# Half A's feed-forward in half B's order: its second product partly by blocks, and eight weight-sum jobs moved beside its later couples

## The chip, the cores and the metric

The kernel runs on one core of one Trainium2 chip. The metric is the device time of one execution in microseconds; the time of a kernel is the median of its runs.

## The reference

One layer of a decoder, on 1024 prompt tokens and 32 sample tokens (8 sequences of 4) that share the weights; a second conditioning of the same form goes with the samples. All is float32. Cut to what matters here:

```
h  = rmsnorm(x) * (1 + sc1) + sh1
u  = h @ w_in                                  # x, gate, q, k, v, r, low rank, two merge gates
y_a = rg_lru(conv(u_x)) * gelu(u_g)            # D_RNN 1280, ten blocks of 128
y_b = rmsnorm(chunked_gla(q, k, v, g)) * silu(u_r)
m  = sigmoid(u_ga) * (y_a @ proj_a) + sigmoid(u_gb) * (y_b @ proj_b)
x  = x + gt1 * (m @ w_out)
h2 = rmsnorm(x) * (1 + sc2) + sh2
f1, f2 = split(h2 @ ffn_w1)                    # 1024 -> 2 x 2816
x  = x + gt2 * ((silu(f1) * f2) @ ffn_w2)      # 2816 -> 1024
```

The outputs are the normalised x and the new states of the convolution, the RG-LRU and the GLA.

## The kernel before

**Halves and products.** The tokens are worked in two halves, one after the other: half A (names end in a) is the first 512 prompt tokens, half B (names in b) the other 512 and the 32 samples. Activations lie transposed, features on partitions, tokens in the free dimension. Each float32 product is three TensorE matmuls of split parts (high by high, high by low, low by high). A weight tile is loaded by SP's queue into one of five raw buffers, and `split_w` (L151) makes the parts in one of three "hl" buffers: a copy on ScalarE (L154) and a subtraction on VectorE (L155).

**The feed-forward.** The 2816 hidden features are 22 tiles of 128, each made by a couple of weight tiles (`ffn1`, one column tile for f1 and one for f2). In the whole form (`pair`, `ffn2`) a product is matmuls of 512 columns, three for each k-tile. In the block form (`ffn1_fast`, `ffn2_fast`, with `products` at L1410) a 2 x 2 block scheme makes seven half-size products instead of eight; a couple is then 7 x 4 x 3 = 84 matmuls of 256 columns (tiles fapsa, fbpsa, fcpsa) in place of 96 halves, and the four output couples of `ffn2_fast` are 4 x 7 x 3 x 3 = 252 matmuls (tiles that print as gapsa, gbpsa and gcpsa, like the gates of merge_a; L1472, on six k-tiles). The block form needs sums of the activations (`block_sums`, and `keep` for the hidden tiles) and sums of the weights.

**The weight sums.** They are made while half A runs and stored in device memory, for half A's last couples, for half B's first product (wsum, one for each couple), for its gates (wsumg) and for its second product (wsumf). Two generators make them, one step at each `next` in the places that the main program chooses:

- `weight_sums` (L348), the raw jobs: SP loads two tiles of 128 x 1024, VectorE makes four sums of 128 x 512 (L352 to L355), POOL's queue stores both.
- `paced_sums` (L362), the half-size jobs: POOL copies one column of a pace tile into each of two buffers (L387), which holds the load back to a place in the program; POOL's queue loads both (L388), VectorE makes four sums of 128 x 256 or 128 x 384 (L392 to L396), POOL's queue stores both (L398). The buffers are the tag "sums", two in all, so one job takes both; the copy also waits for the old store from its buffer. The first sum takes the tile that is loaded second.

**Order.** The order on each engine is the order of the code, shaped by generators that are mixed (`mix`, `weave`) and by `high_priority`, which lets splits and some ScalarE copies move ahead. VectorE, ScalarE, POOL and SP each work through their queue in order. Large activations live in 17 slots of the pool "S", smaller ones in 8 of the pool "X" (`xp`).

**Half A before.** `merge_b` (L1182) makes eight columns of gate and y_b product; between them the generator `lru` finishes the last RG-LRU blocks, with the root of blocks 8 and 9 (L1155) and the scan (L1129). `merge_a` (L1271) makes eight columns of gate (gapsa) and y_a product (papsa, two weight tiles pa0a and pa1a). `back` (L1618) does w_out, the norm and the feed-forward: couples 0 to 5 whole (`ffn1_first`, `ffn1`, tiles f1psa, f2psa, f1psa4None ...), couples 6 to 10 by blocks, the whole `ffn2` of k-tiles 0 to 10 (tile f3psa), and from the main program couples 11 to 21 by blocks, then `ffn2` of k-tiles 11 to 21. Half B has in its `back` one `ffn2` of k-tiles 0 to 3 and then `ffn2_fast` twice.

**Jobs before.** Raw jobs for couples 6 to 21: at columns 1 to 7 of `merge_b`, at five columns of `merge_a`, and four in the first `ffn2`. Half-size jobs: two steps at each of columns 4 to 7 of half A's `merge_b` (couples 4 and 5), four jobs for wsumf in `merge_a`, and in half B the rest.

Of the kernel before, what the change touches and what calls it, by code (L numbers as in the profile page):

```python
# [15 lines left out]
P = 128  # L16
D = 1024
KD = 8
# [9 lines left out]
LEVELS = (64, 32, 16, 8, 4, 2, 1)  # L28
EPS = 1e-6
EARLY = 4  # L30
FAST = (6, 4)
KF = (3, 2, 1, 0, 4, 6, 8, 5, 7, 9, 10, 12, 14, 11, 13, 15, 16, 17, 18, 19, 20, 21)
KORD = (0, 2, 4, 6, 1, 3, 5, 7)
GATES = KD // 2
# [20 lines left out]
def hybrid_layer(ctx, tc, I, O):  # L55
# [25 lines left out]
    tp = ctx.enter_context(tc.tile_pool(name="tp", bufs=6))  # L81
    axp = ctx.enter_context(tc.tile_pool(name="axp", bufs=2, space=PSUM))
    drp = ctx.enter_context(tc.tile_pool(name="drp", bufs=1, space=bass.MemoryType.DRAM))
    wsum = {f: drp.tile([P, 2048], F32, name=f"wsum{f}") for f in range(FAST[1], NF)}
    wsumg = [drp.tile([P, 2048], F32, name=f"wsumg{c}") for c in range(GATES)]
    wsum2 = {(q, g): drp.tile([P, 1536], F32, name=f"wsumf{q}{g}") for q in range(4) for g in range(2)}

# [3 lines left out]
    def T(name, w=544):  # L91
        return tp.tile([P, w], F32, tag="t", name=name)
# [254 lines left out]

    def weight_sums():  # L348

        for f in range(FAST[0], NF):  # L350
            r1, r2 = load_raw(I["ffn1"][2 * f], 1024, f"s1{f}"), load_raw(I["ffn1"][2 * f + 1], 1024, f"s2{f}")
            dve.tensor_add(r2[:, 512:1024], r2[:, 0:512], r2[:, 512:1024])  # L352
            dve.tensor_sub(r2[:, 0:512], r1[:, 0:512], r2[:, 0:512])
            dve.tensor_sub(r1[:, 0:512], r2[:, 512:1024], r1[:, 0:512])
            dve.tensor_sub(r1[:, 512:1024], r1[:, 512:1024], r1[:, 0:512])  # L355
            pool.dma_start(wsum[f][:, 0:1024], r1)
            pool.dma_start(wsum[f][:, 1024:2048], r2)
            yield 1
# [3 lines left out]
    def paced_sums():  # L362
# [11 lines left out]
                to = [halves(wsum2[q, g][:, v * 768:(v + 1) * 768], 384, 0) for v in range(2)]  # L374
                jobs.append((384, [halves(I["ffn2"][2 * q + v][:, c:c + 768], 384, 0) for v in range(2)], to))

        for f in range(FAST[1], FAST[0]):
            columns(wsum[f], [I["ffn1"][2 * f + v] for v in range(2)])
        rows(0)
        for c in range(GATES):  # L380
            columns(wsumg[c], [I["w_in"][T_GA + 2 * c + v] for v in range(2)])
        rows(1)
# [20 lines left out]
    class Half:  # L403
        def __init__(s, hf):
            s.hf, s.N = hf, WID[hf]
            s.n = "ab"[hf]

            s.whole = (0, s.N, None, None)
            s.parts = [(0, 256, 0, 0), (256, 256, 0, 256)] if hf == 0 else [(0, 272, 0, 0), (272, 272, 1, 0)]
            s.tiled = None if hf == 0 else [(0, 256, 0, 0), (256, 288, 1, 0)]  # L410
            s.halves = s.parts if hf == 0 else [(o, w, 0, 0) for o, w, _, _ in s.parts]
            s.adas = ada_rest() if hf == 0 else iter(())
            s.early = {}
            s.lr_raw = None
# [673 lines left out]
        def lru_gate(s, nb, m, xc):  # L1088
# [8 lines left out]
                for o, p in s.over(t, g):  # L1097
                    act.activation(o, p, AF.Tanh, scale=0.5, bias=vh[:, b:b + 1])
            dve.scalar_tensor_tensor(ti[:, :N], ti[:, :N], 1.0, xc[:, :N], op0=OP.add, op1=OP.mult)
            if s.hf == 0 or nb < NR - 1:  # L1100
                both = S("la" + n)
                a, hh = both[:, :N], both[:, 544:544 + N]
            else:
                a, hh = [xp.tile([P, 544], F32, tag="X", name=k + n)[:, :N] for k in ("la", "lh")]
# [77 lines left out]
        def merge_b(s):  # L1182
# [14 lines left out]
            for j in range(KD):  # L1197
                n = f"{s.n}{j}"
                if j + lag < KD:
                    first(j + lag)  # L1200
                    yield 5.2
                tg = tgs.pop(j)
                p2 = s.wide("pbps" + n)
                s.gemm(p2, load_w(I["proj_b"][j], 1024, "pb" + n), 8, s.y_b)
                m = xp.tile([P, 544], F32, tag="X", name="mb" + n)
                for (t, p), (o, _) in zip(s.over(tg, p2), s.over(m, p2)):
                    dve.scalar_tensor_tensor(o, t, 1.0, p, op0=OP.add, op1=OP.mult)
                s.mb.append(m)
                pace[0] = tg
                if s.hf == 0 and j:  # L1210
                    next(sums_of, None)
                if s.hf or j >= 4:
                    next(sums_late, None)
                    next(sums_late, None)
                yield 5.2

        def gate_a(s, j):
# [53 lines left out]
        def merge_a(s):  # L1271
            s.m = []
            for j in range(KD):
                tg = s.gate_a(j)
                s.join(j, tg, s.over(tg, s.branch_a(j)))
                s.keep_m(j)
                next(sums_late, None)
                if j % 3 < 2 and j < 7:
                    next(sums_of, None)

# [161 lines left out]
        def keep(s, f, tg):  # L1442

            N, W = s.N, s.N // 2
            if not (s.hf and 4 <= f < 16):
                a = s.act[f] = S(f"fa{s.n}{f}", F32R)
                split(a, tg[:, :N], N)
                return
# [23 lines left out]
        def ffn2_fast(s, g):  # L1472
# [11 lines left out]
            def onto(j, v):  # L1484
                x, samples = s.x[j], lambda t: t[:, HP:N].rearrange("p (b t) -> p b t", t=TS)
                dve.scalar_tensor_tensor(x[:, :HP], v[:, :HP], gains[:, 3, j, 0:1], x[:, :HP], op0=OP.mult, op1=OP.add)
                fx = cp.tile([P, NB, TS], F32, tag="fx", name=f"fx{s.n}{g}{j}", bufs=2)
                dve.tensor_mul(fx, samples(v), bc(gains[:, 3, j, 1:9].unsqueeze(2), [P, NB, TS]))
                dve.tensor_add(samples(x), fx, samples(x))
# [26 lines left out]
        def ffn1_fast(s, fs):  # L1516
# [9 lines left out]
            for f in fs:  # L1526
                n = f"{s.n}{f}"
                pa, pb, pc = [mm(f"f{c}ps{n}")[:, 0, :W] for c in "abc"]
                v1, v2 = T("va" + n), T("vb" + n)
                tg = s.kept(f) if s.hf and f < 16 and f % 2 == 0 else T("ft" + n)  # L1530
                hi, lo, nn = slice(0, W), slice(W, N), slice(0, N)
                product(pa, "11", True)
                s.snap(v1[:, lo], pa)
# [2 lines left out]
                product(pa, "t2", False)  # L1536
                s.snap(v1[:, hi], pa)
                product(pb, "22", False)
                yield 6
                product(pa, "t3", False)  # L1540
                s.snap(v2[:, hi], pa)
# [9 lines left out]
                if s.hf and f == 16:  # L1551
                    s.late = tg
                else:
                    s.keep(f, tg)
                yield 4.5
            as_written(begin, (mybir.EngineType.PE,))

        def ffn1_first(s, part, n):
            for f in range(n) if part[0] == 0 else range(n - 1, -1, -1):
                if part[0] == 0:  # L1560
                    s.act[f] = S(f"fa{s.n}{f}", F32R)
                yield from s.pair(f, part, s.act[f])

        def ffn1(s, fs):
            for f in fs:
                a = s.act[f] = S(f"fa{s.n}{f}", F32R)
                yield from s.pair(f, s.whole, a)

        def ffn2(s, k0, k1, part, acc=None):
            chunks = [(c, min(6, k1 - c)) for c in range(k0, k1, 6)]  # L1570
# [47 lines left out]
        def back(s):  # L1618
# [13 lines left out]
            mix(s.norm2(p1, a1), f)  # L1632
            drain(f)
            b = s.block_sums(s.h2)
            if s.hf == 0:
                mix(chain(s.ffn1_first(p1, EARLY), s.ffn1(range(EARLY, FAST[0]))), b)
                drain(b)
                drain(s.ffn1_fast(range(FAST[0], 11)))
                for j, _ in enumerate(s.ffn2(0, 11, s.whole)):
                    if j % 2 == 0:  # L1640
                        next(sums_of, None)
                return
            s.fs = {k: [] for k in ("11", "21", "22", "t1", "t2", "t3", "t4")}
            mix(chain(s.ffn1_first(p1, EARLY), s.ffn2(0, 4, s.whole)), b)
            drain(b)
            drain(s.ffn1_fast(range(4, 11)))
            drain(s.ffn2_fast(0))
            drain(s.ffn1_fast(range(11, 17)))
            drain(s.ffn2_fast(1))
            s.keep(16, s.late)  # L1650
# [39 lines left out]
    derive()  # L1690
    A.branches(None)
    drain(sums_of)
    A.act = {}
    drain(A.ffn1_fast(range(11, NF)))
    acc = [ACC("3a")]
    dn = A.ffn2(11, NF, A.whole, acc)
    next(dn)
    B.load_x(pool)
    mix(chain(B.norm1_sum(), B.norm1()), dn)
# [117 lines left out]
```

## Time and profile before

| what | value |
|---|---|
| time, median of 3 runs (range) | 1961.64 us (1959.43 to 1966.48) |
| the profiled execution: its time, its span | 1964.05 us, 1962.3 us |
| mean granted TensorE clock | 0.994 |
| VectorE busy | 1361.2 us (69%) |
| ScalarE busy | 972.8 us (50%) |
| DMA moved | 319.24 MB, mean 163 GB/s |

The span is from the first to the last instruction. Times in a row are microseconds from the start of the span; a row of the timeline is start, duration, engine, line, operation, output and inputs by the program's names, shapes, and in brackets the idle time of the engine before it with what ended that. TensorE's matmuls are pipelined, so their spacing is told by the starts. A row of the windows is from:to, its length, then the busy time of PE, its weight load, VectorE, ScalarE and POOL, each with its count of instructions, the granted clock as a share of the full one, the share of the DMA engines and GB/s.

### The profile page before, as it was taken

How to read it: one execution, taken by the hardware profiler on the slowest of the kernel's cores; microseconds unless marked ns; L12 is line 12 of the kernel's file. 1: busy time of each engine (PE TensorE's matmuls, PEld its weight loads, DVE VectorE, ACT ScalarE, POOL GpSimd, SP SyncE). 2: the span in 40 equal slices, each digit the busy share in tenths (PEclk: the TensorE clock that was granted, in tenths of full speed). 3: DMA queues.
4: the chain of work that ended last, by engine and by line, in shares of the span. 5: the costliest groups of instructions: out<-in, count | busy, mean ns of one | idle time of the engine just before them, and what ended most of it. 6: DMA issues, size and time to landing. Idle time of an engine off the chain costs nothing. (4 is left out here: it accounts for less than half of the span.)

```text
span 1962.3 us, 33970 instructions
## 1 busy us (share of the span) xinstructions
PE 1928.1 (98%) x13380; PEld 1756.9 (90%) x13380; DVE 1361.2 (69%) x2420; ACT 972.8 (50%) x1559; POOL 148.8 (8%) x279
## 2 busy tenths in 40 slices
PE   9999999998999999999999999999999999999997
PEld 5877777786899998999899998999999999999997
DVE  5648587666658774677674497786467688888867
ACT  4536376533235552555353365665245354666653
POOL 0000001122100000000000001141201000000000
PEclk9999999998999999999999999999999999999999
DMA  8344325476764456554332412334446634555553
GB/s 341 116 154 175 117 92 197 153 262 250 267 227 156 129 179 234 196 185 156 118 119 68 145 50 88 127 121 141 146 140 228 202 130 130 176 169 180 176 164 105
DMA packets 122241, 319.24 MB, mean 163 GB/s; under 512 B 14561, under 2 KB 29665, under 8 KB 122081
## 3 DMA queue, kind: packets, MB, share of 16 engines
q1 hardware_dynamic: 107536, 263.89, 41.5%
q0 software_dynamic: 14000, 52.62, 7.4%
q8 instruction: 105, 1.72, 0.4%
q10 hardware_dynamic: 544, 0.56, 0.1%
q14 instruction: 56, 0.45, 0.1%
HBM read 278.42 MB, written 38.59 MB: 162 GB/s over the span
## 5 line engine op out<-in xcount | busy, mean ns | idle before, releaser
L155 DVE TENSOR_TENSOR fwa_hl<-fwa,fwa_hl 128x1024 fp32r<-128x1024 f32 (+1 forms) x57 | 68.8, 1207 | 44.4 <-ACT fwa_hl L154 43.8
L155 DVE TENSOR_TENSOR fwb_hl<-fwb,fwb_hl 128x1024 fp32r<-128x1024 f32 (+1 forms) x64 | 77.2, 1207 | 27.4 <-ACT fwb_hl L154 27.1
L154 ACT ACTIVATE fwa_hl<-fwa 128x1024 fp32r<-128x1024 f32 (+1 forms) x57 | 59.3, 1040 | 43.7 <-PE fapsa L1431 10.7
L154 ACT ACTIVATE fwb_hl<-fwb 128x1024 fp32r<-128x1024 f32 (+1 forms) x64 | 66.6, 1041 | 23.4 <-PE fcpsb L1431 9.0
L454 PE MATMUL f3psa<-faa,f3a_hl 128*128 128x512 f32 x176 | 68.7, 391 | 1.2 <-DVE f3a_hl L155 1.2
L452 PE MATMUL f3psa<-faa,f3a_hl 128*128 128x512 f32 x176 | 68.7, 390 | 0.6 <-ACT f3a_hl L154 0.6
L453 PE MATMUL f3psa<-faa,f3a_hl 128*128 128x512 f32 x176 | 68.6, 390 | 0.0
L154 ACT ACTIVATE f3a_hl<-f3a_raw 128x768 fp32r<-128x768 f32 (+1 forms) x32 | 25.3, 792 | 56.7 <-PE f3psa L454 37.8
L352 DVE TENSOR_TENSOR s_raw<-s_raw 128x512 f32<-128x512 f32 x16 | 11.1, 692 | 49.3 <-DMA s_raw<-in_ffn 49.3
L454 PEld LDWEIGHTS f3psa<-faa,f3a_hl 128*128 128x128 f32 x176 | 33.0, 188 | 8.9 <-DVE f3a_hl L155 2.1
L452 PEld LDWEIGHTS f3psa<-faa,f3a_hl 128*128 128x128 f32 x176 | 33.0, 188 | 7.7 <-ACT f3a_hl L154 1.0
L453 PEld LDWEIGHTS f3psa<-faa,f3a_hl 128*128 128x128 f32 x176 | 33.1, 188 | 6.8
L155 DVE TENSOR_TENSOR f3a_hl<-f3a_raw,f3a_hl 128x768 fp32r<-128x768 f32 (+1 forms) x32 | 28.3, 888 | 14.3 <-ACT f3a_hl L154 14.3
L454 PE MATMUL wopsb<-mb,wob_hl 128*128 128x272 f32 x128 | 36.9, 288 | 0.0
L452 PE MATMUL wopsb<-mb,wob_hl 128*128 128x272 f32 x128 | 36.9, 289 | 0.0
L453 PE MATMUL wopsb<-mb,wob_hl 128*128 128x272 f32 x128 | 36.8, 288 | 0.0
L453 PE MATMUL wopsa<-ma,woa_hl 128*128 128x256 f32 x128 | 36.4, 284 | 0.0
L454 PE MATMUL wopsa<-ma,woa_hl 128*128 128x256 f32 x128 | 36.2, 283 | 0.0
L452 PE MATMUL wopsa<-ma,woa_hl 128*128 128x256 f32 x128 | 36.1, 283 | 0.0
L1616 POOL DMA_DIRECT2D out_yb<-yb x4 | 2.9, 720 | 407.6 <-DVE yb L1613 406.9
L452 PE MATMUL uxpsa<-h1a,uxpsa_hl 128*128 128x512 f32 x80 | 32.3, 403 | 0.0
L155 DVE TENSOR_TENSOR fvb_hl<-fvb,fvb_hl 128x768 fp32r<-128x768 f32 x28 | 26.8, 956 | 7.7 <-ACT fvb_hl L154 7.3
(2402 smaller groups left out, 7986.7 us busy)
## 6 DMA issues: line engine op xcount, KB each, us to landing
ada<-in_ada_w SPq DMA_DIRECT2D x48, 512.0 KB, 5.5
fwb<-wsum SPq DMA_DIRECT2D x72, 256.0 KB, 3.6
s_raw<-in_ffn SPq DMA_DIRECT2D x32, 512.0 KB, 4.8
wsum<-s_raw POOLq DMA_DIRECT2D x32, 512.0 KB, 3.8
fwa<-wsum SPq DMA_DIRECT2D x64, 256.0 KB, 3.4
fwb<-in_ffn SPq DMA_DIRECT2D x54, 256.0 KB, 3.7
fwa<-in_ffn SPq DMA_DIRECT2D x48, 256.0 KB, 3.2
woa_raw<-in_w_out SPq DMA_DIRECT2D x13, 512.0 KB, 3.6
```

The costliest lines, as they stand in the source:

```text
L154: act.activation(hl[:, 0, :n], raw[:, :n], AF.Copy)
L155: dve.tensor_sub(hl[:, 1, :n], raw[:, :n], hl[:, 0, :n].bitcast(F32))
L352: dve.tensor_add(r2[:, 512:1024], r2[:, 0:512], r2[:, 512:1024])
L452: pe.matmul(out, wh, x[:, o:o + w], start=st, stop=False)
L453: pe.matmul(out, wh, x[:, N + o:N + o + w], start=False, stop=False)
L454: pe.matmul(out, wl, x[:, o:o + w], start=False, stop=en)
L1616: (queues[j // 2 % len(queues)]).dma_start(out[:, j:j + 2, o:o + w], y2)
```

## The change

- **Half A's feed-forward takes half B's order.** `FAST = (6, 4)` becomes `RAW, BLOCKS = (6, 18), (10, 16)`. In `back`, half A now does couples 0 to 3 with the whole `ffn2` of k-tiles 0 to 3, couples 4 to 10 by blocks, and `ffn2_fast(0)` on k-tiles 4 to 9; then the main program does couples 11 to 21 by blocks and the whole `ffn2` of k-tiles 10 to 21. `keep` makes the block parts for half A's tiles 4 to 9.
- **Raw jobs** are those of couples 6 to 17: columns 0 to 6 of `merge_b` and five of `merge_a`. There are none in a whole `ffn2`.
- **Half-size jobs** are two-phase at each place: a first `next` issues the loads, a second, later in the same column or couple, the sums and stores. Those of couples 4 and 5 stand at columns 3 to 6 of `merge_b`, those of wsumf at columns 1 to 4 of `merge_a`. Eight new ones, for couples 18 to 21, stand in the last `ffn1_fast` of half A beside couples 12 to 19, paced by the result of the couple before (`fta`).
- **RG-LRU block 9** of half A has its decay and state (`la`, `lh`) in the pool "X", as half B has, and not in a slot of "S".

The matmuls of the kernel go from 12606 to 12786: f3psa from 528 to 384, the whole couples 4 and 5 from 192 to none, 168 more of a block couple, 252 of the second product.

```diff
-FAST = (6, 4)
+RAW, BLOCKS = (6, 18), (10, 16)
...
-        for f in range(FAST[0], NF):
+        for f in range(*RAW):
...
-        for f in range(FAST[1], FAST[0]):
-            columns(wsum[f], [I["ffn1"][2 * f + v] for v in range(2)])
+        def pairs(fs):
+            for f in fs:
+                columns(wsum[f], [I["ffn1"][2 * f + v] for v in range(2)])
+
+        pairs(range(EARLY, RAW[0]))
         rows(0)
+        pairs(range(RAW[1], NF))
...
-            if s.hf == 0 or nb < NR - 1:
+            if nb < NR - 1:
                 both = S("la" + n)
...
                     first(j + lag)
+                if s.hf or 3 <= j < 7:
+                    pace[0] = tgs[j]
+                    next(sums_late, None)
+                if j + lag < KD:
                     yield 5.2
...
-                pace[0] = tg
-                if s.hf == 0 and j:
+                if s.hf or 3 <= j < 7:
+                    next(sums_late, None)
+                if s.hf == 0 and j < 7:
                     next(sums_of, None)
-                if s.hf or j >= 4:
-                    next(sums_late, None)
-                    next(sums_late, None)
...
                 tg = s.gate_a(j)
+                if 1 <= j < 5:
+                    next(sums_late, None)
                 s.join(j, tg, s.over(tg, s.branch_a(j)))
                 s.keep_m(j)
-                next(sums_late, None)
+                if 1 <= j < 5:
+                    next(sums_late, None)
...
-            if not (s.hf and 4 <= f < 16):
+            if not EARLY <= f < s.blocks:
...
                 product(pb, "22", False)
+                late = s.hf == 0 and 12 <= f < 20
+                if late:
+                    next(sums_late, None)
                 yield 6
...
                     s.keep(f, tg)
+                if late:
+                    next(sums_late, None)
+                pace[0] = tg
                 yield 4.5
...
-            if s.hf == 0:
-                mix(chain(s.ffn1_first(p1, EARLY), s.ffn1(range(EARLY, FAST[0]))), b)
-                drain(b)
-                drain(s.ffn1_fast(range(FAST[0], 11)))
-                for j, _ in enumerate(s.ffn2(0, 11, s.whole)):
-                    if j % 2 == 0:
-                        next(sums_of, None)
-                return
             s.fs = {k: [] for k in ("11", "21", "22", "t1", "t2", "t3", "t4")}
             mix(chain(s.ffn1_first(p1, EARLY), s.ffn2(0, 4, s.whole)), b)
             drain(b)
             drain(s.ffn1_fast(range(4, 11)))
             drain(s.ffn2_fast(0))
+            if s.hf == 0:
+                return
...
-    dn = A.ffn2(11, NF, A.whole, acc)
+    dn = A.ffn2(10, NF, A.whole, acc)
```

In the changed kernel the lines behind L402 are four to fourteen higher; L392 to L398 of the half-size jobs are L396 to L402 there, and L1550 is L1564.

**ScalarE at the end of half A's merge_b.** laa is the decay of RG-LRU block 9 (lma holds the squares of blocks 8 and 9 for the root), gba a gate of merge_b, pa0a and pa1a the weights of merge_a's first column. Before:

```order
L1098 ACTIVATE tia_3418<-g2a_3414,vh 128x512
L1192 ACTIVATE gba_3458<-gbpsa_3428 128x512
...
L154 ACTIVATE pa0a_hl<-pa0a_raw 128x640
L1106 ACTIVATE laa_3422<-tra_3417,sp_147 128x512
L1192 ACTIVATE gba_3630<-gbpsa_3600 128x512
L1107 ACTIVATE tra_3417<-tra_3417,sp_147 128x512
L1108 ACTIVATE lma_3394<-laa_3422 128x512
L1155 ACT_TABLE_LOAD
L1155 ACTIVATE lma_3394<-lma_3394 128x1024
L154 ACTIVATE pa1a_hl<-pa1a_raw 128x640
```

And now:

```order
L1102 ACTIVATE tia_3440<-g2a_3436,vh 128x512
L1110 ACTIVATE laa_3444<-tra_3439,sp_147 128x512
L1111 ACTIVATE tra_3439<-tra_3439,sp_147 128x512
L1112 ACTIVATE lma_3416<-laa_3444 128x512
L1159 ACT_TABLE_LOAD
L1159 ACTIVATE lma_3416<-lma_3416 128x1024
L1196 ACT_TABLE_LOAD
L1196 ACTIVATE gba_3481<-gbpsa_3451 128x512
```

The decay, the square and the root moved from between the two weight splits of merge_a's first column to ahead of the gate that is the second row before.

**VectorE in the last ffn1_fast of half A.** fta is the result of a couple, faa its kept split, fwa_hl the split of the next weights, vaa and vba parts of the next couple. From the result of couple 12 on, before:

```order
L1550 TENSOR_TENSOR fta_7029<-fta_7029,fapsa_7024 128x256
L155 TENSOR_TENSOR fwa_hl<-fwa_7252,fwa_hl 128x1024
L189 TENSOR_TENSOR faa_7143<-fta_7029,faa_7143 128x512
L1542 TENSOR_TENSOR vaa_7149<-vaa_7149,fbpsa_7147 128x256
L155 TENSOR_TENSOR fwa_hl<-fwa_7293,fwa_hl 128x1024
L1545 TENSOR_TENSOR vba_7150<-vba_7150 128x256
```

And now:

```order
L1564 TENSOR_TENSOR fta_7326<-fta_7326,fapsa_7321 128x256
L155 TENSOR_TENSOR fwa_hl<-fwa_7567,fwa_hl 128x1024
L189 TENSOR_TENSOR faa_7446<-fta_7326,faa_7446 128x512
L396 TENSOR_TENSOR sums_7391<-sums_7391 128x256
L1556 TENSOR_TENSOR vaa_7458<-vaa_7458,fbpsa_7456 128x256
L398 TENSOR_TENSOR sums_7391<-sums_7390,sums_7391 128x256
L155 TENSOR_TENSOR fwa_hl<-fwa_7614,fwa_hl 128x1024
L399 TENSOR_TENSOR sums_7390<-sums_7391,sums_7390 128x256
L1559 TENSOR_TENSOR vba_7459<-vba_7459 128x256
L400 TENSOR_TENSOR sums_7390<-sums_7390 128x256
```

The four sums of a job now stand in the queue behind the keep, the first of them ahead of the next weight split.

**POOL's queue in the same stage.** xb is half B's input, wsum_92 to wsum_95 the stores of couples 18 to 21. Before, from the first whole ffn2 on:

```order
L357 DMA wsum_94<-s_raw 128x1024
L356 DMA wsum_94<-s_raw 128x1024
L357 DMA wsum_95<-s_raw 128x1024
L356 DMA wsum_95<-s_raw 128x1024
L541 DMA xb_8321<-in_xb 128x1088
```

And now, the first two of the eight jobs:

```order
L391 COPY sums_7390<-fta_7198 128x1
L391 COPY sums_7391<-fta_7198 128x1
L392 DMA sums_7390<-in_ffn 128x2x256
L392 DMA sums_7391<-in_ffn 128x2x256
L402 DMA wsum_92<-sums_7391 128x2x256
L402 DMA wsum_92<-sums_7390 128x2x256
L391 COPY sums_7524<-fta_7326 128x1
L392 DMA sums_7524<-in_ffn 128x2x256
L391 COPY sums_7525<-fta_7326 128x1
L392 DMA sums_7525<-in_ffn 128x2x256
```

The loads of a job stand behind the stores of the job before, each behind a copy into its own buffer.

More of the change, by code (lines that the diff above doesn't have):

```diff
@@ L83, in hybrid_layer @@
     drp = ctx.enter_context(tc.tile_pool(name="drp", bufs=1, space=bass.MemoryType.DRAM))
-    wsum = {f: drp.tile([P, 2048], F32, name=f"wsum{f}") for f in range(FAST[1], NF)}
+    wsum = {f: drp.tile([P, 2048], F32, name=f"wsum{f}") for f in range(EARLY, NF)}
     wsumg = [drp.tile([P, 2048], F32, name=f"wsumg{c}") for c in range(GATES)]
@@ L405, in __init__ @@
             s.hf, s.N = hf, WID[hf]
-            s.n = "ab"[hf]
+            s.n, s.blocks = "ab"[hf], BLOCKS[hf]
             s.whole = (0, s.N, None, None)
@@ L1529, in ffn1_fast @@
                 v1, v2 = T("va" + n), T("vb" + n)
-                tg = s.kept(f) if s.hf and f < 16 and f % 2 == 0 else T("ft" + n)
+                tg = s.kept(f) if f < s.blocks and f % 2 == 0 else T("ft" + n)
                 hi, lo, nn = slice(0, W), slice(W, N), slice(0, N)
@@ L1562, in ffn1_first @@
                 yield from s.pair(f, part, s.act[f])
[L1564 to L1567, printed above, removed]
         def ffn2(s, k0, k1, part, acc=None):
@@ L1647, in back @@
             drain(s.ffn2_fast(0))
+            if s.hf == 0:
+                return
             drain(s.ffn1_fast(range(11, 17)))
@@ L1692, in hybrid_layer @@
     drain(sums_of)
-    A.act = {}
     drain(A.ffn1_fast(range(11, NF)))
     acc = [ACC("3a")]
-    dn = A.ffn2(11, NF, A.whole, acc)
+    dn = A.ffn2(10, NF, A.whole, acc)
     next(dn)
```

## Prediction

> **What bounds the kernel now.** I read the page's busy times and slices first, then TensorE's own rows in order of time, then the DMA view and the rows of one job. The page:
>
> ```profile
> span 1962.3 us, 33970 instructions
> PE 1928.1 (98%) x13380; PEld 1756.9 (90%) x13380; DVE 1361.2 (69%) x2420; ACT 972.8 (50%) x1559; POOL 148.8 (8%) x279
> PE   9999999998999999999999999999999999999997
> PEclk9999999998999999999999999999999999999999
> ```
>
> TensorE is busy for 98% of the span, so a change pays in two ways only: fewer TensorE microseconds, or less of the 34 us in which it waits. In the slices PE and its clock both fall short in the tenth alone (442 to 491 us). There stands the one large gap, between the two projections of half A's merge_a, column 0. TensorE's rows at it, and those of the next column beside them:
>
> ```profile
> 458.11 0.39 PE L452 MATMUL papsa<-yaa,pa0a_hl 128*128 128x512 f32 x1
> 469.74 0.80 PE L454 MATMUL papsa<-yaa,pa1a_hl 128*128 128x512 f32 x1 [7.48 <-DVE pa1a_hl L155]
> 475.46 0.52 PE L452 MATMUL gapsa<-h1a,gapsa_hl 128*128 128x512 f32 x1
> 481.05 0.39 PE L452 MATMUL papsa<-yaa,pa0a_hl 128*128 128x512 f32 x1
> 487.85 0.39 PE L452 MATMUL gapsa<-h1a,gapsa_hl 128*128 128x512 f32 x1
> 452.00:482.00 30.00, 22.52 (x87) 17.87 (x86) 20.81 (x33) 11.58 (x15) 13.56 (x16) 0.83 0.59 200
> ```
>
> Column 0 takes 475.46 - 458.11 = 17.35 us, column 1 takes 487.85 - 481.05 = 6.80 us for the same matmuls: the gap costs **10.6 us**, 7.48 of it idle and the rest at the lower granted clock (0.83 in the window's row) behind it. Who was late, on ScalarE and VectorE:
>
> ```profile
> 456.66 0.60 ACT L1192 ACTIVATE gba<-gbpsa 128x512 f32<-128x512 f32 x1 [7.73 <-DVE mba L1207]
> 459.79 1.06 ACT L1155 ACTIVATE lma<-lma 128x1024 f32<-128x1024 f32 x1
> 460.76 0.72 ACT L154 ACTIVATE pa1a_hl<-pa1a_raw 128x640 fp32r<-128x640 f32 x1
> 463.75 0.43 DVE L392 TENSOR_TENSOR sums<-sums 128x256 f32<-128x256 f32 x1 [3.95 <-DMA sums<-in_ffn]
> 468.87 0.82 DVE L155 TENSOR_TENSOR pa1a_hl<-pa1a_raw,pa1a_hl 128x640 fp32r<-128x640 f32 x1
> ```
>
> ScalarE reaches the square root of LRU blocks 8 and 9 (L1155) late, behind a gate (L1192) that waited 7.73 us; VectorE then waits 3.95 us for the load of a half-size job, and only after that do the scan and the split of pa1a follow.
>
> **The change part by part.** First the two products that move to blocks, from the starts of TensorE's matmuls:
>
> ```profile
> 659.37 0.40 PE L452 MATMUL f1psa4None<-h2a,f1a4None_hl 128*128 128x512 f32 x1
> 681.16 0.28 PE L1429 MATMUL fapsa<-h2a,fwa_hl 128*128 128x256 f32 x1
> 792.41 0.28 PE L1429 MATMUL fapsa<-h2a,fwa_hl 128*128 128x256 f32 x1
> 903.06 0.40 PE L452 MATMUL f3psa<-faa,f3a_hl 128*128 128x512 f32 x1
> ```
>
> Couples 4 and 5 are now 96 matmuls of 512 columns in 681.16 - 659.37 = 21.79 us, 0.227 each. The last 11 couples by blocks take (903.06 - 792.41)/11 = 10.06 us each: 84 matmuls, 0.1197 each.
>
> - Couples 4 and 5 by blocks: 2 x 10.06 - 21.79 = **-1.7 us**.
> - Second product: k-tiles 4 to 9 leave the whole form, 144 x 0.227 = 32.7 us, and come back as 252 half-width matmuls, 30.2 us: **-2.5 us**. Its own weight sums are four jobs that were done already, now in merge_a.
> - The gap: block 9 of half A no longer waits for a slot of the large pool, so its exponential, root and scan stand ahead of the last gate in the order, and no job is summed between column 7 of merge_b and column 0 of merge_a. I take the whole gap as gone: **-10.6 us**. What is late next there is the split of pa1a itself, 0.72 on ScalarE and 0.82 on VectorE, under the 5.6 us that a column's gate matmuls take (475.46 to 481.05). The cover would fail if the jobs now at columns 3 to 6 pushed VectorE as this one did; that is a rival.
> - Four raw jobs fewer in the first `ffn2` (they become half-size jobs, next), and block sums, keeps and snaps of half A beside TensorE. VectorE's load in such a stage is 58.28 of 80 us (the row of 804 to 884 us below); I cost them at nothing.
>
> What remains is the eight new jobs beside couples 12 to 19 of the last `ffn1_fast`. VectorE's queue is in order. A job's first sum waits there for the job's loads, and the split of the next weights (fwa_hl, L155) that TensorE needs stands behind it. The sums buffers are two, and one job takes both, so jobs form a loop: first sum, four sums, store, its landing, POOL's copy, load, its landing, the next first sum. The loop has run in before, in half B's merge_b:
>
> ```profile
> 1382.35 0.42 DVE L392 TENSOR_TENSOR sums<-sums 128x256 f32<-128x256 f32 x1
> 1384.73 0.43 DVE L396 TENSOR_TENSOR sums<-sums 128x256 f32<-128x256 f32 x1
> 1394.86 0.42 DVE L392 TENSOR_TENSOR sums<-sums 128x256 f32<-128x256 f32 x1 [0.48 <-DMA sums<-in_w_in]
> 1385.45 0.73 POOL L398 DMA_DIRECT2D wsumg<-sums  x1 [1.21 <-DVE sums L396]
> 1389.13 0.19 POOL L387 COPY sums<-gbb 128x1 f32<-128x1 f32 x1 [0.89 <-DMA wsumg<-sums]
> 1389.37 1.43 POOL L388 DMA_DIRECT2D sums<-in_w_in  x2
> 1406.24 0.42 DVE L392 TENSOR_TENSOR sums<-sums 128x256 f32<-128x256 f32 x1
> ```
>
> Sum to sum is 1394.86 - 1382.35 = 12.5 us, and a DMA ends it; store to copy is 3.68, load (the second one's issue, 0.72 behind the first) to sum 4.77. The next turn there was 1406.24 - 1394.86 = 11.4. In half A's merge_b the traffic is heavier:
>
> ```profile
> 417.49 0.42 DVE L392 TENSOR_TENSOR sums<-sums 128x256 f32<-128x256 f32 x1
> 419.58 0.73 POOL L398 DMA_DIRECT2D wsum<-sums  x1 [0.20 <-issue]
> 424.57 0.18 POOL L387 COPY sums<-gba 128x1 f32<-128x1 f32 x1 [4.26 <-DMA wsum<-sums]
> 426.70 0.73 POOL L388 DMA_DIRECT2D sums<-in_ffn  x1 [0.31 <-POOL sums L387]
> 433.23 0.42 DVE L392 TENSOR_TENSOR sums<-sums 128x256 f32<-128x256 f32 x1
> 1394.00:1432.00 38.00, 38.00 (x308) 38.00 (x307) 20.85 (x41) 9.36 (x15) 9.70 (x18) 1.00 0.43 137
> 411.00:452.00 41.00, 41.00 (x176) 32.61 (x175) 24.01 (x36) 14.66 (x20) 8.07 (x14) 1.00 0.80 285
> 804.00:884.00 80.00, 80.00 (x670) 80.00 (x669) 58.28 (x85) 47.16 (x76) 0.00 (x0) 1.00 0.58 183
> DMA to landing us min/median/max: 2.5/4.0/6.8
> ```
>
> The last columns of a window's row are the share of the DMA engines and GB/s; the last row is the landing of every DMA of the sums tiles. Under 285 GB/s the loop was 15.7 us, with 4.99 from store to copy. The new stage has 183 GB/s without jobs. Slowed to 13 us a couple that is 142, and a job's four transfers of 256 KB in 13 us add 81: some 220 GB/s, between the two stages and nearer the second. Store to copy then comes to about 4.6, load to sum to about 5.8 (4.77, and at 285 GB/s at most 6.5, from the load's issue at 426.70); with 2.8 for the sums and their issue, 0.3 and 0.2 for waits of POOL and the copy, and 0.7 off because the loads are now issued one by one as each store lands, an estimate of **13 us**. A couple offers 10.06. VectorE itself is not the limit: 58.28/80 x 10.06 + 4 x 0.42 = 9.0 us.
>
> - Seven turns between the first and the eighth job: 7 x (13 - 10.06) = **+20.6 us**. TensorE's lead over VectorE's splits can hide the first turn or so, but not the place of the eighth sum, from which the next term counts.
> - The eighth job makes couple 21's weights, and is summed during couple 20. The natural place of a sum is behind the keep of the couple before:
>
> ```profile
> 818.11 0.68 DVE L189 TENSOR_TENSOR faa<-fta,faa 128x512 fp32r<-128x512 f32 x1
> fwa<-wsum SPq DMA_DIRECT2D x64, 256.0 KB, 3.4
> 812.72 1.06 ACT L154 ACTIVATE fwa_hl<-fwa 128x1024 fp32r<-128x1024 f32 x1 [1.54 <-PE fapsa L1431]
> 813.81 1.23 DVE L155 TENSOR_TENSOR fwa_hl<-fwa,fwa_hl 128x1024 fp32r<-128x1024 f32 x1 [1.04 <-ACT fwa_hl L154]
> ```
>
> That couple began at 792.41 + 2 x 10.06 = 812.53 and the keep ended at 818.8, 6.3 us in, so 3.8 us are left to the next couple. SP's load of couple 21's first weights waits for the store, with all of SP's later loads behind it: two sums 0.9, 0.3, store 4.6, load 3.4, split 2.3 = 11.5 us, so **+7.7 us** of idle TensorE.
>
> The sum: -1.7 - 2.5 - 10.6 + 20.6 + 7.7 = +13.5 us, against the profiled execution's 1964.05 us; that run lies 2.4 above the median of the runs shown, so I put the same difference on the median: 1961.64 + 13.5 = **1975 us**. With the shortest turn seen (11.4, store 3.7) the last two terms are 9.4 + 6.8 and the time 1963; with the longest (15.7, store 5.0) 39.5 + 8.1 and 1994. I take 13 because the stage's traffic lies between the two stages.
>
> **Rivals.**
>
> (A) The loop fits into the couple, and only the last term stays: -14.8 + 6.8 = -8, so 1954. It decides at a turn of 10.06 us: with both landings at the shortest of the row above, 2.5, a turn is 2.8 + 0.3 + 0.72 + 2.5 + 0.2 + 0.72 + 2.5 = 9.7. For it speaks that minimum and that the second turn of half B was only 11.4; against it, that the median landing is 4.0 and that no turn in the trace is that short. The Trainium skill, "DMA: Bandwidth & Descriptors", section on the anatomy of one DMA on the GpSimd path, fits a DMA's time as 2.0 us plus its bytes over 436 KB per us, 2.6 us for 256 KB: by that price too the loop would fit. The trace's row above, 4.0 at the median, speaks against it here. 0.18.
>
> (B) The gap in merge_a stays, at another column: four jobs stand now at columns 3 to 6 of merge_b and four at 1 to 4 of merge_a, each with a wait like the 3.95 us above. Then -10.6 is lost: 1986. Against it: the root and scan are ahead of it all. 0.12.
>
> (C) Everything is hidden, the eighth store too, because ScalarE and VectorE run far enough ahead: -14.8, so 1947. Against it: two buffers. 0.08.
>
> **How the numbers follow.** My case has 0.62, and 1975 is its middle. A measurement of this kernel can tell about 0.5%, 9.8 us, from no change: 1951.8 and 1971.4. Faster are C and somewhat under half of A: 0.15. Within the bound are the rest of A and my case with turns under about 12.5 us: 0.35. Slower are the rest of my case and B: 0.50. The range leaves out C at the one end and the longest turns at the other: 1950 to 1992.
>
> **What would show it.** In the changed profile: 384 f3psa matmuls, 252 of the new second product, no papsa row with a wait of over 2 us. In the last `ffn1_fast`, starts of couples 13 us apart from couple 14 on, VectorE's first sum waiting about 3 us for its load in each, POOL's copy waiting for a store, and one TensorE gap of 5 to 8 us ahead of couple 21. I am wrong if the couples keep 10.06 us, if the first sums show no DMA wait, or if the gap at papsa is there.

## The result, and the profile after

| | before | changed |
|---|---|---|
| time, median of 6 runs each (range) | 1964.02 us (1959.43 to 1967.16) | 1988.24 us (1985.36 to 1992.52) |
| the profiled execution: its time, its span | 1964.05, 1962.3 us | 1989.06, 1987.2 us |

The ratio is 1.0129, with a 95% interval of 1.0116 to 1.0143: the change makes the kernel 24 us slower. The forecast was 13.5 us slower, so the direction holds and the size does not. The forecast put its 13.5 us on 1961.64, a median of three runs; the six runs here have 1964.02, so its 1975 lies only 11 us above them. The page of the changed kernel:

```profile
span 1987.2 us, 34584 instructions
PE 1933.9 (97%) x13560; PEld 1770.5 (89%) x13560; DVE 1387.9 (70%) x2491; ACT 993.6 (50%) x1602; POOL 172.6 (9%) x319
PE   9999999999999999888999999999999999999997
PEclk9999999999999999998999999999999999999999
```

TensorE's busy time was 34 us less than the span before the change, and is 53 us less now. The hole in the tenth slice is gone from this row, and a new one stands in slices 17 to 19, the last `ffn1_fast` of half A. TensorE's rows there, the starts of couples 11, 15, 16, 20 and 21 and of the `ffn2` behind them:

```profile
776.66 0.28 PE L1438 MATMUL fapsa<-h2a,fwa_hl 128*128 128x256 f32 x1
...
816.90 0.28 PE L1438 MATMUL fapsa<-h2a,fwa_hl 128*128 128x256 f32 x1
831.31 0.28 PE L1438 MATMUL fapsa<-h2a,fwa_hl 128*128 128x256 f32 x1
...
889.20 0.28 PE L1438 MATMUL fapsa<-h2a,fwa_hl 128*128 128x256 f32 x1
908.12 0.58 PE L1438 MATMUL fapsa<-h2a,fwa_hl 128*128 128x256 f32 x1 [5.89 <-ACT fwa_hl L154]
921.77 0.40 PE L456 MATMUL f3psa<-faa,f3a_hl 128*128 128x512 f32 x1
```

Couples 11 to 14 take 10.06 us each. Couple 15 takes 831.31 - 816.90 = 14.4 us, couple 20 takes 18.9 with the wait ahead of couple 21 in it, and couple 21 itself 13.65. VectorE and POOL's queue in the same stretch, from the third job's sums (L400 is the last of the four) to the fourth job's first, and the eighth job's first; the last row is the landing of all DMAs of the sums tiles from 800 to 910 us:

```profile
833.60 0.43 DVE L396 TENSOR_TENSOR sums<-sums 128x256 f32<-128x256 f32 x1 [6.28 <-DMA sums<-in_ffn]
836.41 0.42 DVE L400 TENSOR_TENSOR sums<-sums 128x256 f32<-128x256 f32 x1
837.13 0.73 POOL L402 DMA_DIRECT2D wsum<-sums  x1 [1.42 <-DVE sums L400]
841.08 0.40 POOL L391 COPY sums<-fta 128x1 f32<-128x1 f32 x1 [1.12 <-DMA wsum<-sums]
842.06 0.72 POOL L392 DMA_DIRECT2D sums<-in_ffn  x1 [0.59 <-POOL sums L391]
846.89 0.43 DVE L396 TENSOR_TENSOR sums<-sums 128x256 f32<-128x256 f32 x1 [5.46 <-DMA sums<-in_ffn]
900.22 0.43 DVE L396 TENSOR_TENSOR sums<-sums 128x256 f32<-128x256 f32 x1 [3.24 <-DMA sums<-in_ffn]
DMA to landing us min/median/max: 2.5/4.3/7.0
```

This is the loop, step by step: four sums, store, the copy that waits for the store to land, load, and a first sum that waits for the load while the weight splits stand behind it (3.2 to 6.4 us in the seven turns). The eight first sums lie at 803.0, 818.1, 833.6, 846.9, 862.0, 875.1, 889.1 and 900.2: seven turns of 13.9 us on average. By the same rows of all seven, the means of the parts are 3.35 us from the first sum to the last store's issue, 4.76 to POOL's copy, 1.00 to the load's issue and 4.78 to the next first sum.

In merge_a the wait has moved rather than gone. TensorE and VectorE there, at the gate of column 1:

```profile
468.87 0.80 PE L458 MATMUL gapsa<-h1a,gapsa_hl 128*128 128x512 f32 x1 [3.62 <-DVE gapsa_hl L155]
465.53 0.69 DVE L352 TENSOR_TENSOR s_raw<-s_raw 128x512 f32<-128x512 f32 x1 [6.70 <-DMA s_raw<-in_ffn]
467.59 1.22 DVE L155 TENSOR_TENSOR gapsa_hl<-gapsa_raw,gapsa_hl 128x1024 fp32r<-128x1024 f32 x1
556.75 0.28 PE L456 MATMUL wopsa<-ma,woa_hl 128*128 128x256 f32 x1
```

There is no wait at papsa, but VectorE waits 6.70 us for the load of the raw job of column 0, with the gate's split behind it. In the kernel before, the split of that gate came ahead of the job's first sum, which waited 0.59 us; the third row is the first wopsa there:

```profile
471.14 1.22 DVE L155 TENSOR_TENSOR gapsa_hl<-gapsa_raw,gapsa_hl 128x1024 fp32r<-128x1024 f32 x1
473.75 0.69 DVE L352 TENSOR_TENSOR s_raw<-s_raw 128x512 f32<-128x512 f32 x1 [0.59 <-DMA s_raw<-in_ffn]
562.00 0.28 PE L452 MATMUL wopsa<-ma,woa_hl 128*128 128x256 f32 x1
```

merge_a ends (the first wopsa, w_out's first matmul) at 556.75 against 562.00 before: 5.25 us earlier, half of what the old gap had cost.

Laid over the two profiled executions, which differ by 24.9 us in their spans: 5.25 less up to the end of merge_a, 5.5 less for the two products that went to blocks, 34.5 more in couples 11 to 21, 1.2 more in half B.

### The profile page after: what moved, and what is told of

It reads as the page before. It is cut to its first block, busy times and chain, and to the rows that moved or that the text cites. A ratio compares the mean times of both kernels' runs of the same rounds, so it can differ in the third digit from the quotient of the medians.

```text
span 1987.2 us, 34584 instructions
## 1 busy us (share of the span) xinstructions
PE 1933.9 (97%) x13560; PEld 1770.5 (89%) x13560; DVE 1387.9 (70%) x2491; ACT 993.6 (50%) x1602; POOL 172.6 (9%) x319
## 5 line engine op out<-in xcount | busy, mean ns | idle before, releaser
L155 DVE TENSOR_TENSOR fwa_hl<-fwa,fwa_hl 128x1024 fp32r<-128x1024 f32 (+1 forms) x64 | 77.2, 1206 | 26.9 <-ACT fwa_hl L154 26.8
L154 ACT ACTIVATE fwa_hl<-fwa 128x1024 fp32r<-128x1024 f32 (+1 forms) x64 | 66.6, 1041 | 38.4 <-PE fapsa L1440 10.8
L456 PE MATMUL f3psa<-faa,f3a_hl 128*128 128x512 f32 x128 | 49.9, 391 | 0.9 <-ACT f3a_hl L154 0.9
L457 PE MATMUL f3psa<-faa,f3a_hl 128*128 128x512 f32 x128 | 50.0, 390 | 0.0
L458 PE MATMUL f3psa<-faa,f3a_hl 128*128 128x512 f32 x128 | 49.9, 390 | 0.0
L396 DVE TENSOR_TENSOR sums<-sums 128x256 f32<-128x256 f32 (+1 forms) x28 | 12.9, 459 | 42.8 <-DMA sums<-in_ffn 42.4
L154 ACT ACTIVATE f3a_hl<-f3a_raw 128x768 fp32r<-128x768 f32 (+1 forms) x24 | 18.5, 773 | 30.7 <-PE f3psa L458 22.0
L391 POOL COPY sums<-fta 128x1 f32<-128x1 f32 x16 | 10.4, 655 | 269.2 <-ACT vaa L1446 254.5
L456 PE MATMUL uxpsa<-h1a,uxpsa_hl 128*128 128x512 f32 x80 | 32.3, 403 | 0.0
L155 DVE TENSOR_TENSOR fvb_hl<-fvb,fvb_hl 128x768 fp32r<-128x768 f32 x28 | 26.8, 956 | 7.7 <-ACT fvb_hl L154 7.4
L457 PE MATMUL uxpsa<-h1a,uxpsa_hl 128*128 128x512 f32 x80 | 31.2, 390 | 0.0
L458 PE MATMUL uxpsa<-h1a,uxpsa_hl 128*128 128x512 f32 x80 | 31.2, 390 | 0.0
L456 PE MATMUL ugpsa<-h1a,ugpsa_hl 128*128 128x512 f32 x80 | 31.1, 389 | 0.0
```

What stands on the lines that cost most here:

```text
L154: act.activation(hl[:, 0, :n], raw[:, :n], AF.Copy)
L155: dve.tensor_sub(hl[:, 1, :n], raw[:, :n], hl[:, 0, :n].bitcast(F32))
L391: pool.tensor_copy(r[v][:, 0:1], pace[0][:, 0:1])
L396: dve.tensor_add(r2[:, 1], r2[:, 0], r2[:, 1])
L456: pe.matmul(out, wh, x[:, o:o + w], start=st, stop=False)
L457: pe.matmul(out, wh, x[:, N + o:N + o + w], start=False, stop=False)
```

## Experiments

The theory was the prediction's, with its sizes corrected: the eight jobs form a loop through two buffers that is longer than a couple, the last store is needed too early, and in merge_a a raw job waits where a half-size job had waited. Against it stood the block form itself, the work of the jobs in VectorE and DMA traffic, and the loads alone. In what follows "before" is the kernel before on the same chip.

**Without the late jobs.**

```diff
+    wsum.update({f: wsum[f - 8] for f in range(18, NF)})
-        pairs(range(RAW[1], NF))
-                late = s.hf == 0 and 12 <= f < 20
+                late = False
```

> Left out: the eight half-size jobs beside couples 12 to 19 of half A; couples 18 to 21 of both halves read the weight sums of couples 10 to 13 in their place. Theory (the loop of sum, store, load through the two sums buffers is the whole loss): the couples are back at 10.06 us each, the 34.6 us that they and couple 21 took too long are gone, and the time is 1988 - 35 = 1953 us, 1951 to 1957. Rival (the block form itself overloads VectorE, SP or the DMA engines in half A, whatever the jobs): couples stay above 11 us and the time above 1965.

Measured: 1955.6 us against 1962.5, ratio 0.9961 (0.9948 to 0.9975). The starts of couples 12 and 21 and of the `ffn2` behind them:

```profile
786.41 0.28 PE L1438 MATMUL fapsa<-h2a,fwa_hl 128*128 128x256 f32 x1
...
876.95 0.28 PE L1438 MATMUL fapsa<-h2a,fwa_hl 128*128 128x256 f32 x1
887.01 0.40 PE L456 MATMUL f3psa<-faa,f3a_hl 128*128 128x512 f32 x1
```

Nine couples in 90.54 us are 10.06 each. So the rest of the change is worth 7 us, and the jobs beside the couples cost 31 (24 + 7). The block form is not the cause.

**The late jobs without their stores.**

```diff
+    wsum.update({f: wsum[f - 8] for f in range(18, NF)})
-            for v in range(2):
+            for v in range(0 if 8 <= k < 16 else 2):
                 pool.dma_start(to[v], rv[v])
```

> Left out: the stores of the eight late jobs; couples 18 to 21 of both halves read the sums of couples 10 to 13. Loads, POOL's copies and sums stay. Theory (the store and its landing, 4.9 us of a turn of 13.9, are in the loop): a turn is about 9 us and fits, first sums wait under 1 us, 1953 to 1960. Rival (the loads alone, slowed by traffic and by POOL's copies, set the pace): first sums still wait 3 us or more and the time is 1975 or more.

Measured: 1956.1 us, ratio 0.9972 (0.9963 to 0.9981). Two of the first sums:

```profile
811.93 0.42 DVE L397 TENSOR_TENSOR sums<-sums 128x256 f32<-128x256 f32 x1 [1.27 <-DMA sums<-in_ffn]
823.01 0.43 DVE L397 TENSOR_TENSOR sums<-sums 128x256 f32<-128x256 f32 x1 [0.92 <-DMA sums<-in_ffn]
```

Such waits come to 12.6 us over the stretch, against 36.3 in the changed kernel, and a turn falls from 13.9 to 10.5 us on average, just over a couple. All loads, copies and sums are there, so their work costs next to nothing: the loss arises only with the stores. The time is as the theory has it, the turn of 9 us and the waits under 1 us are not: the waits are 0.9 to 2.9 us. Without the stores there is also less traffic; the run with four buffers below has all of it.

**Four jobs, at every second couple.**

```diff
+    wsum.update({f: wsum[f - 8] for f in range(20, NF)})
-        pairs(range(RAW[1], NF))
+        pairs(range(RAW[1], 20))
-                late = s.hf == 0 and 12 <= f < 20
+                late = s.hf == 0 and f in (12, 14, 16, 18)
```

> Left out: four of the eight jobs; the other four stand beside couples 12, 14, 16 and 18, and couples 20 and 21 of both halves read the sums of couples 12 and 13. Theory (loop): a turn of 14 us has 20.1 us, so no first sum waits over 1 us and the couples stay at 10.06: 1953 to 1958 us. Rival (each job costs its 4.3 us in VectorE time, POOL copies and DMA traffic, however far apart): half of the 34.6 us stays, 1971.

Measured: 1971.3 us, ratio 1.0041 (1.0027 to 1.0055). The number is the rival's, the trace is not. A first sum, and the only gap in the stretch:

```profile
825.86 0.42 DVE L397 TENSOR_TENSOR sums<-sums 128x256 f32<-128x256 f32 x1
870.80 0.58 PE L1439 MATMUL fapsa<-h2a,fwa_hl 128*128 128x256 f32 x1 [10.72 <-ACT fwa_hl L155]
```

No first sum waits for a DMA, and couples 11 to 17 take 10.06 us each. The loss sits in one place: the fourth job, placed at couple 18, is summed at 862.6 us, when couple 18's matmuls are over, and couple 19 needs its result at once. TensorE waits 10.72 us, and the couple behind it takes 3.0 us too long at the lower clock. The edit had put the store too late, which the expectation overlooked; without these 14 us the time would be 1957. So jobs 20 us apart are free, and a store that comes a couple late has a price of its own.

**All eight jobs one couple earlier.**

```diff
-                late = s.hf == 0 and 12 <= f < 20
+                late = s.hf == 0 and 11 <= f < 19
```

> All eight jobs, beside couples 11 to 18 in place of 12 to 19. Theory (loop, and a separate last wait for the eighth store): the seven turns stay at about 14 us, but couple 21's first weights come a couple earlier, so the gap of 5.9 us ahead of couple 21 and the slow clock behind it, some 8 us, go: 1980, 1978 to 1983. Rival (the last wait is only the end of the loop, whatever its place): 1988.

Measured: 1982.2 us, ratio 1.0101 (1.0086 to 1.0116), as the theory has it. Couple 21 and what follows:

```profile
904.33 0.28 PE L1438 MATMUL fapsa<-h2a,fwa_hl 128*128 128x256 f32 x1
914.39 0.40 PE L456 MATMUL f3psa<-faa,f3a_hl 128*128 128x512 f32 x1
```

Couple 21 starts without a wait and takes 10.06 us. The turns stay at 14.2 us. The loop and the last store are two costs, about 26 and 6 us.

**Half the width.**

```diff
...
+            if 8 <= k < 16:
+                rv, src, to = [[t[:, :, :128] for t in ts] for ts in (rv, src, to)]
```

> The changed kernel with late jobs of half the width: 128 columns of each 256 are loaded, summed and stored, and no couple waits for these stores, since couples 18 to 21 of both halves read the sums of couples 10 to 13. Left out: the other half of the eight jobs. Theory (a turn is mostly the fixed part of two landings): a turn falls from 13.9 only to 11.5 to 12.5, and the time to 1965 to 1973. Rival (a turn goes with the bytes): it fits into the couple, 1955 to 1960.

Measured: 1968.0 us, ratio 1.0031 (1.0018 to 1.0043). The DMAs of the sums tiles from 790 to 905 us, and a sum:

```profile
DMA to landing us min/median/max: 2.2/3.7/5.8
L400 DVE TENSOR_TENSOR sums<-sums x8: 289/292/293, 802.7 to 887.5; 128x128 f32<-128x128 f32 x8
```

Half the bytes take the landing from 4.3 to 3.7 us at the median and the turn from 13.9 to 12.1, of which the four shorter sums are 4 x 0.13 = 0.5. Half the bytes save 1.8 us of the turn, so most of it does not go with the size. The Trainium skill, "DMA: Bandwidth & Descriptors", section on the anatomy of one DMA on the GpSimd path, says the same in form: a fixed part of 2.0 us that is mostly the confirmation that the last byte has landed, plus bytes over 436 KB per us. The estimate by its figures for 256 KB, 2.6 us, is near the shortest landing here (2.5), not the median; the measured 4.3 decides.

**Four buffers.** The jobs of odd number get a pair of their own; the raw buffers go from five to four, in both places that take one, to make room.

```diff
+            if 8 <= k < 16 and k % 2:
+                r = [wp.tile([P, 512], F32, tag="late", name=f"sums{k}{v}", bufs=2) for v in range(2)]
+            else:
+                r = [wp.tile([P, 768], F32, tag="sums", name=f"sums{k}{v}", bufs=2) for v in range(2)]
```

> The changed kernel with two more buffers: the late jobs of odd number take a pair of their own (the raw buffers are four in place of five to make room). Theory (a job waits for the store of the job before only through its buffer): each pair has two couples, 20 us, for a turn of 14, no first sum waits over 1 us, the couples stay at 10.06; the wait of couple 21 for the eighth store stays, 4 us and a slow clock behind it: 1958 to 1965. Rival (the jobs' DMA and VectorE work is what costs): 1980 or more.

Measured: 1961.4 us, ratio 0.9992 (0.9979 to 1.0005). A first sum, and TensorE at couples 19 and 21:

```profile
853.41 0.42 DVE L399 TENSOR_TENSOR sums<-sums 128x256 f32<-128x256 f32 x1
869.16 0.39 PE L1441 MATMUL fapsa<-t4a,fwa_hl 128*128 128x256 f32 x1 [1.72 <-ACT vba L1449]
885.14 0.38 PE L1441 MATMUL fapsa<-h2a,fwa_hl 128*128 128x256 f32 x1 [2.74 <-ACT fwa_hl L154]
```

No first sum waits for a DMA; the same jobs with the same traffic go along with couples of 10.06 us up to couple 18. What stays are the waits at couples 19 and 21, and gaps of 1.60 and 2.66 us in merge_a; whether the first two come from late stores is tried below.

**The price of the four raw buffers alone,** on the kernel before:

> The kernel before with four raw buffers in place of five: what the room for the two extra buffers costs by itself. Theory: under 3 us, 1962 to 1966. Rival (the raw buffers carry the loads' lead everywhere): 1970 or more, and then the four-buffer kernel hides a larger gain.

```diff
-        raw = wp.tile([P, 1024], F32, tag="raw", name=name + "_raw", bufs=5)
+        raw = wp.tile([P, 1024], F32, tag="raw", name=name + "_raw", bufs=4)
```

Measured: 1959.3 us, ratio 0.9986 (0.9975 to 0.9997). They cost nothing; the time even lies below the range expected.

**Four buffers and one couple earlier.**

> The four-buffer kernel with the eight late jobs beside couples 11 to 18 in place of 12 to 19; nothing is left out. Theory (with the loop gone, what is left are the waits of couples 20 and 21 for stores that come one couple too late, 6.4 us before the couples' starts and 2.8 us in couple 21): 1961.4 - 9 = 1952 to 1956 us, faster than the kernel before by 0.4 to 0.6%. Rival (the waits come from the four raw buffers, not from the stores' place): 1960 or more.

```diff
-                late = s.hf == 0 and 12 <= f < 20
+                late = s.hf == 0 and 11 <= f < 19
```

Measured: 1953.4 us, ratio 0.9959 (0.9946 to 0.9971): faster than both kernels, with nothing left out. The stretch as a whole, and merge_a:

```profile
784.00:885.00 101.00, 101.00 (x845) 100.99 (x844) 83.28 (x138) 59.03 (x97) 26.50 (x48) 1.00 0.82 265
451.76:554.74 102.98, 100.33 (x435) 82.22 (x434) 59.70 (x87) 28.21 (x39) 17.85 (x36) 0.98 0.79 274
```

TensorE has no idle time from couple 12 to 21, with VectorE at 83.28 of 101 us and the DMA engines at 0.82, more than in the changed kernel (0.62 from 816.9 to 889.2). Neither VectorE's load nor the traffic was the limit.

**The raw job of merge_a's column 0 moved.**

```diff
-                if j % 3 < 2 and j < 7:
+                if j in (1, 3, 4, 5, 6):
                     next(sums_of, None)
```

> The changed kernel with one edit: the raw job at column 0 of half A's merge_a stands at column 5. Theory (the half of the gap that stayed in merge_a is VectorE's 6.70 us wait for that raw job's load, ahead of the next gate's split): the 3.6 us gap and the slow clock behind it go, 5 us in all: 1983. Rival (the traffic of that stretch makes whatever stands next wait as long): no change, 1988.

Measured: 1991.0 us, ratio 1.0145 (1.0128 to 1.0162), no better than the changed kernel. The gap at column 1 is gone, and two others have come:

```profile
517.90 0.79 PE L458 MATMUL gapsa<-h1a,gapsa_hl 128*128 128x512 f32 x1 [3.94 <-DVE gapsa_hl L155]
535.34 0.50 PE L458 MATMUL gapsa<-h1a,gapsa_hl 128*128 128x512 f32 x1 [2.10 <-DVE gapsa_hl L155]
516.02 0.69 DVE L352 TENSOR_TENSOR s_raw<-s_raw 128x512 f32<-128x512 f32 x1 [4.90 <-DMA s_raw<-in_ffn]
```

Four columns in a row now carry a raw job, and the loads are late at two of them (by 4.90 us in the last row, by 3.79 ahead of the second gap). The rival was right that no time is won: the wait goes with the jobs, not with column 0.

**No raw jobs in merge_a,** on the kernel with four buffers one couple earlier:

```diff
+    wsum.update({f: wsum[f - 5] for f in range(13, 18)})
-        for f in range(*RAW):
+        for f in range(RAW[0], 13):
```

> The same as the run with four buffers one couple earlier, and left out: the five raw jobs in half A's merge_a; couples 13 to 17 of both halves read the sums of couples 8 to 12. Theory (the raw jobs' loads, waited for in VectorE's queue ahead of the gate's splits, are what costs in merge_a): no gap of over 1 us there and 4 to 6 us less than with them, 1948 to 1951. Rival (the half-size jobs at columns 1 to 4 or something else there makes the gap): no less than 1 us of difference.

Measured: 1946.2 us against 1953.4, ratio to before 0.9920 (0.9909 to 0.9932) against 0.9959; 7.2 us less, more than the 4 to 6 expected. merge_a in the windows, and VectorE's longest wait in the merge_a of the kernel with the raw jobs:

```profile
452.39:550.47 98.08, 98.08 (x435) 81.24 (x434) 49.33 (x68) 29.01 (x39) 12.17 (x26) 1.00 0.53 180
508.08 0.69 DVE L352 TENSOR_TENSOR s_raw<-s_raw 128x512 f32<-128x512 f32 x1 [6.68 <-DMA s_raw<-in_ffn]
```

TensorE is busy without a break and at the full clock in 98.08 us, against 102.98 with the raw jobs. The half-size jobs at columns 1 to 4 are still there, so it is the raw jobs that cost there. That they do so by the wait for their loads is read from VectorE's rows; what their sums, stores and traffic cost by themselves was not tried.

**Block 9 alone,** on the kernel before:

```diff
-            if s.hf == 0 or nb < NR - 1:
+            if nb < NR - 1:
```

> The kernel before with one edit: block 9 of half A in the pool X. Theory (the root and scan of block 9 were late for want of a slot, and the half-size job ahead of them only rode along): the 7.5 us gap between papsa's projections goes, and a gap at the next gate, behind a raw job, may stay, so 5 to 10 us less than before, 1953 to 1958. Rival (the job at column 7 alone made the wait): the gap stays, 1962.

Measured: 1962.0 us against 1963.4, ratio 0.9995 (0.9984 to 1.0006): no change, so the theory missed. TensorE's two gaps there, and VectorE's wait ahead of the second:

```profile
459.69 0.50 PE L454 MATMUL papsa<-yaa,pa0a_hl 128*128 128x512 f32 x1 [0.84 <-DVE pa0a_hl L155]
472.26 0.79 PE L454 MATMUL gapsa<-h1a,gapsa_hl 128*128 128x512 f32 x1 [5.43 <-DVE gapsa_hl L155]
470.38 0.69 DVE L352 TENSOR_TENSOR s_raw<-s_raw 128x512 f32<-128x512 f32 x1 [7.53 <-DMA s_raw<-in_ffn]
```

The old gap is gone, so the slot was its cause; behind it stands the raw job's gap, which takes most of it back (merge_a ends 2.2 us earlier).

**The last four pairs as raw jobs in the first block stretch.**

```diff
-RAW, BLOCKS = (6, 18), (10, 16)
+RAW, BLOCKS = (6, 22), (10, 16)
-                late = s.hf == 0 and 12 <= f < 20
+                late = False
-                if j % 3 < 2 and j < 7:
+                if j in (1, 3, 4, 5, 6):
...
                 pace[0] = tg
+                if s.hf == 0 and f in (4, 6, 8, 10):
+                    next(sums_of, None)
```

> The changed kernel without late half-size jobs: couples 18 to 21 are raw jobs again, beside couples 4, 6, 8 and 10 in half A's first block stretch, and the raw job of merge_a's column 0 stands at column 5. Nothing is left out. Theory (the loop of the two sums buffers and the raw job in merge_a are all that kept the gain away): 1955.6 of the run without the late jobs, less 5: 1951, 1948 to 1954. Rival (any weight sums beside couples cost TensorE time, by VectorE's load of 7.3 + 2.8 of 10.06 us and DMA traffic): couples of the first stretch grow by some us, 1960 or more.

Measured: 1965.4 us, ratio 1.0017 (1.0007 to 1.0028). One of the gaps in that stretch, and in merge_a:

```profile
735.13 0.39 PE L1438 MATMUL fapsa<-t4a,fwa_hl 128*128 128x256 f32 x1 [2.56 <-ACT vba L1446]
536.26 0.79 PE L458 MATMUL gapsa<-h1a,gapsa_hl 128*128 128x512 f32 x1 [4.10 <-DVE gapsa_hl L155]
```

It lost in both places: the couples of the stretch took up to 13.2 us, as the rival had it, and the edit in merge_a that was no help above is in this kernel too. The expectation had counted that edit as a gain.

## Why the prediction came out as it did

Two steps failed: the gap in merge_a was taken as wholly gone, and a turn of the loop was taken as too short. The mechanism of the largest term, the loop, was right.

- **Two products by blocks, -4.2 us.** Near: 5.5 less. From the end of merge_a to couple 11 the changed kernel takes 219.91 us against 230.41, and the last `ffn2` with its one k-tile more 68.8 against 63.9. The whole couples 4 and 5 were 96 matmuls, as the prediction counts them; the 192 in the section on the change is twice that.
- **The gap in merge_a, -10.6 us.** This step failed by half: -5.25. The prediction said that no job is summed between column 7 of merge_b and column 0 of merge_a, and asked what is late next only of pa1a's split. The raw job at column 0 now stands ahead of the next gate's split in VectorE's queue, and its load came 6.70 us late. The job was in the kernel before as well, but behind that split, with a wait of 0.59 us; the run with block 9 alone has it ahead of the split, with a wait of 7.53 us, so the wait came with the new place of block 9. Rival (B) had the gap at another column and gave it to the half-size jobs; the run without raw jobs in merge_a shows whose it is. That (B)'s 1986 lies near the measured 1988 is luck: half of the old gap did go, and the turns cost 6.2 us more than forecast.
- **Seven turns, +20.6 us.** The mechanism is shown (stores left out, four buffers), the size was low: a turn is 13.9 us, not 13, and seven of them take 26.8 us more than seven couples. The couples were slow from 15 on, not 14, and the first sums waited 5.2 us on average, not 3. By its parts: sums to store 3.35 us (3.1 assumed), store to copy 4.76 (4.6), load to sum 4.78 (5.8, less the 0.7), all near; what was missed is POOL's step from the copy to the load's issue, 1.00 us where 0.2 stood. The traffic was 194 GB/s from 816.9 to 889.2 us, not 220.
- **Couple 21, +7.7 us.** Right in sum, with other parts. From the eighth sum to couple 21 it took 7.9 us, not 11.5, since the store landed after 2.6 and not 4.6; but couple 21 itself took 3.6 us too long at the lower clock, which had no term.
- **Rivals.** (A) is refuted by the traces: the shortest turn of the eight jobs was 11.1 us. So is (C).
- **Half B, +1.2 us,** had no term, and was not followed. From the first matmul behind half A's last `ffn2` to the end of the span it is 995.4 us before and 996.6 after; in the traces of the twelve experiments it lies between 993.2 and 999.9, so 1.2 is within what traces differ by.

The forecast of 13.5 us lacked 5.3 in merge_a, 6.2 in the turns and 1.2 in half B, and gained 1.3 at the products: 24.9.

## What to carry to other kernels

A job that loads, works and stores through one set of buffers turns no faster than its two landings, and a job of half the size turned only 1.8 of 13.9 us faster here; compare the turn with the time that the cover offers, and if it doesn't fit, add a second set of buffers before shrinking the job. Where a wait is removed from an in-order queue, list every instruction in it up to the next one that the bound engine needs, since another wait may take the place of the first. A result that is stored for later needs its own count: sum, landing, load and split, back from the first use.

## What the runs showed of the hardware

A wait of TensorE costs more than its idle time, but not always. After the 5.89 us ahead of couple 21 the matmuls follow each other at 0.21 us instead of 0.12, for 6.6 us:

```profile
909.76 0.41 PE L1438 MATMUL fapsa<-h2a,fwa_hl 128*128 128x256 f32 x1
909.97 0.41 PE L1439 MATMUL fapsa<-h2a,fwa_hl 128*128 128x256 f32 x1
817.20:836.10 18.90, 12.33 (x98) 11.82 (x98) 11.61 (x21) 6.49 (x10) 5.11 (x7) 1.00 0.54 168
836.12:839.53 3.41, 3.40 (x16) 3.10 (x16) 3.38 (x8) 1.85 (x3) 2.11 (x3) 0.50 0.90 268
849.77:853.18 3.41, 3.41 (x19) 3.41 (x18) 3.41 (x6) 0.91 (x2) 2.27 (x3) 0.50 0.79 184
```

The windows are of the same trace. A gap of 3.34 us ends at 820.64, and the granted clock stays at 1.00; gaps of 2.73 and 2.52 us end at 835.88 and 849.42, and each is followed by 3.41 us at 0.50. The Trainium skill, "TensorE: Matmul & The Clock Gate", part 1, explains such a spread: the clock is halved after an idle window of about 3.4 us that runs freely, and comes back after a busy one. The lengths of the two slow spells agree with it; that gaps of 2.73 and 2.52 us among other short ones were enough, and one of 3.34 was not, is only what these rows show.

POOL's copy of one column is the other thing. The groups of the sums tiles have, as shortest, median and longest in ns, for the changed kernel:

```profile
L391 POOL COPY sums<-fta x14: 185/784/1175, 810.0 to 895.5; 128x1 f32<-128x1 f32 x14
```

and for the kernel with four buffers, one couple earlier:

```profile
L394 POOL COPY sums<-fta x12: 179/179/548, 797.9 to 848.9; 128x1 f32<-128x1 f32 x12
```

At the median the same copy takes four times as long in the changed kernel. There it took 0.82 to 1.10 us each time that it stood right behind the issue of a store, and 0.18 to 1.18 where it had waited for a store to land; in the other kernel the copies that had waited for a landing took 0.18 to 0.55. Why was not tried.
